# Passing a matmul's columns in turns: eight orders of the moving columns in 40 tiles of a two-layer expert network

## The chip, the cores and the metric

The kernel runs on one core of one Trainium2 chip. The metric is the device time of one execution in microseconds. Three runs of the kernel before gave 2364.71, 2369.80 and 2374.26 us, with a median of 2369.8 us.

## The reference, cut to what matters

A network of three blocks works on 256 tokens of width 1024 in float32. The part that matters here is the expert layer (`peer_ffn`), which stands behind each of the first two mixers. Every token picks 16 of 16384 experts for each of 8 heads; each expert is one row of `u` and one row of `v`:

```
u = u_tab[expert]
act = jax.nn.gelu(jnp.einsum('thkd,td->thk', u, xc).astype(jnp.float32), approximate=False)
w = (g * act).astype(xc.dtype)
return jnp.einsum('thk,thkd->td', w, v_tab[expert])
```

The kernel doesn't gather the rows. It computes the activations of all 16384 experts, multiplies them by gates that are zero for the experts not picked, and multiplies the result with the whole of `v`: out (256 x 1024) = w (256 x 16384) times v (16384 x 1024). This last product is the v stage.

## The kernel before, in words

All weights stream through one object (`Stream`, `self.ws`). A DMA on SP's queue brings a tile of 128 x 1024 float32 into `raw`; ScalarE copies it, rounded, into the first half of a `parts` buffer (line 103), and VectorE subtracts that from `raw` to give the rest (line 105). There are three `raw` and three `parts` buffers, used in turn. The moving operand of a product is 512 columns of such a part.

Each product of the reference is three products on TensorE (`mm3`, lines 464 to 468): high by high (466), high by low (467), low by high (468), all added up in one PSUM bank. `fp32r` in the profile is the type of the rounded parts.

In the v stage 128 tiles of `v` are taken one after another by `acc_tile`. For each tile the stationary operand is a block of 128 experts by 128 tokens of w, for two halves of the tokens (`tt`); the moving operand is the tile of `v`, in two halves of 512 columns (`hf`). That makes 2 x 2 x 3 = 12 products of 128x512 for a tile, and the sums stay in four PSUM banks of 512 float32 columns each until all 128 tiles are through. The stationary operands come from the array A by ScalarE (line 1124) and VectorE (line 1125), two tiles at a time. In the second half of the stage, which is the one changed, they lie in three pairs of tiles named w; in the first half four of five lie in hT. The second half runs through 60 tiles in the loop of lines 1104 to 1107 and through the last four in `close`.

Nothing here is scheduled by a planner: instructions stand on each engine in the order in which the Python code issues them. Ahead of each tile, `self.ws.get()` issues the splits and loads that are due.

## Time and profile before

| | |
|---|---|
| median of three runs | 2369.8 us (2364.71 to 2374.26) |
| the profiled execution | 2370.52 us |
| span of the profiled execution, first to last instruction | 2368.7 us |
| PE (TensorE matmul) busy | 2326.8 us, 98% of the span, 16813 products |
| DVE (VectorE) busy | 1767.5 us, 75% |
| ACT (ScalarE) busy | 1402.5 us, 59% |
| DMA | 406.90 MB, mean 172 GB/s |

A busy PE means that a product was under way: products are pipelined, so the time of one in the groups is its latency, and what a product costs is the distance from its start to the next one's start. PEld is the load of a stationary operand, which runs beside the products.

### The profile page before, as it was taken

The page shows a single profiled execution, that of the slowest core. Times are in us where ns is not written, and L with a number is a line of the kernel's source. Part 1 is how long each engine was busy: PE and PEld are TensorE (multiplying, and loading weights), DVE is VectorE, ACT ScalarE, POOL GpSimd, SP SyncE. Part 2 cuts the span into 40 slices and gives each one's busy share as a digit, 9 for nine tenths or more (in the row PEclk, how much of TensorE's full clock was granted, in tenths as well). Part 3 has the DMA queues.
Part 4 walks back from the last instruction along what each step waited for, and adds up shares of the span by engine and source line. Part 5 has one row for each costly group of instructions (what it writes and reads, how often), then busy time and mean ns, then how long its engine had stood idle before and what let it go on. Part 6 is the DMA issues. An engine that isn't in the chain of part 4 may idle for free.

```text
span 2368.7 us, 42927 instructions
## 1 busy us (share of the span) xinstructions
PE 2326.8 (98%) x16813; PEld 2082.1 (88%) x16814; DVE 1767.5 (75%) x3378; ACT 1402.5 (59%) x2109; POOL 144.3 (6%) x184
## 2 busy tenths in 40 slices
PE   9999999999999999999999999999999999999998
PEld 6679999999888888878999999888888899997987
DVE  6759997888999555557999788999755645548654
ACT  4554446777877445674445777877644555544543
POOL 1220000000000001121000000000000101215000
PEclk9899999999999999999999999999999999999999
DMA  5345555555555655434555555555556553435554
GB/s 179 107 134 162 191 186 178 177 177 175 183 177 178 197 194 194 157 106 161 169 195 190 183 175 178 181 177 177 197 194 195 177 168 114 158 119 177 187 193 153
DMA packets 113242, 406.90 MB, mean 172 GB/s; under 512 B 13200, under 2 KB 13584, under 8 KB 112784
## 3 DMA queue, kind: packets, MB, share of 16 engines
q1 hardware_dynamic: 112896, 403.91, 52.0%
q8 instruction: 131, 2.15, 0.4%
q14 instruction: 71, 0.58, 0.1%
q10 hardware_dynamic: 144, 0.26, 0.0%
HBM read 403.08 MB, written 1.05 MB: 171 GB/s over the span
## 4 chain that ended last, share of the span: by engine, by line
PE 84%; DVE 11%; issue 2%; ACT 2%; DMA 1%; POOL 1%; POOLq 0%; DVEq 0%; ACTq 0%
PE bank L466 25%; PE bank L468 25%; PE bank L467 25%; DVE parts L105 4%; PE bank L1174 3%; PE bank L740 1%; DVE ri L1211 1%; DVE ri L1214 1%; DVE rw L1212 1%; DVE rv L1213 1%; PE bank L783 1%; PE bank L810 1%; PE bank L739 1%; PE bank L526 1%; DVE rv L1210 1%
## 5 line engine op out<-in xcount | busy, mean ns | idle before, releaser
L105 DVE TENSOR_TENSOR parts<-raw,parts 128x1024 fp32r<-128x1024 f32 (+1 forms) x714 | 871.0, 1224 | 387.9 <-ACT parts L103 386.7
L103 ACT ACTIVATE parts<-raw 128x1024 fp32r<-128x1024 f32 (+2 forms) x726 | 759.3, 1050 | 474.0 <-PE bank L468 317.9
L468 PE MATMUL bank<-hT,parts 128*128 128x256 f32 x2816 | 783.4, 278 | 9.0 <-DVE parts L105 8.7
L466 PE MATMUL bank<-hT,parts 128*128 128x256 f32 x2816 | 789.6, 280 | 0.0
L467 PE MATMUL bank<-hT,parts 128*128 128x256 f32 x2816 | 781.4, 277 | 0.0
L468 PEld LDWEIGHTS bank<-hT,parts 128*128 128x128 f32 x2816 | 528.7, 188 | 12.6 <-DVE parts L105 12.5
L466 PEld LDWEIGHTS bank<-hT,parts 128*128 128x128 f32 x2816 | 529.0, 188 | 5.6 <-issue 3.5
L467 PEld LDWEIGHTS bank<-hT,parts 128*128 128x128 f32 x2816 | 531.8, 189 | 0.1
L466 PE MATMUL bank<-parts,hT 128*128 128x512 f32 (+4 forms) x624 | 240.6, 386 | 0.2 <-ACT parts L103 0.2
L467 PE MATMUL bank<-parts,hT 128*128 128x512 f32 (+4 forms) x624 | 235.9, 378 | 0.8 <-DVE parts L105 0.8
L468 PE MATMUL bank<-parts,hT 128*128 128x512 f32 (+4 forms) x624 | 236.1, 378 | 0.0
L466 PE MATMUL bank<-parts,w 128*128 128x512 f32 x592 | 230.9, 390 | 0.0
L468 PE MATMUL bank<-parts,w 128*128 128x512 f32 x592 | 230.4, 389 | 0.0
L467 PE MATMUL bank<-parts,w 128*128 128x512 f32 x592 | 230.3, 389 | 0.0
L1116 ACT ACTIVATE A<-bank 128x512 f32<-128x512 f32 x128 | 76.6, 598 | 180.4 <-PE bank L468 180.4
L1146 ACT ACTIVATE e<-i2T 128x512 f16<-128x512 f16 x256 | 157.5, 615 | 3.7 <-DVE o L1152 3.1
L1147 ACT ACTIVATE eg<-gT 128x512 f16<-128x512 f16 x256 | 157.4, 615 | 0.0
L466 PEld LDWEIGHTS bank<-parts,hT 128*128 128x128 f32 x624 | 117.3, 188 | 21.3 <-issue 1.7
L468 PEld LDWEIGHTS bank<-parts,hT 128*128 128x128 f32 x624 | 117.2, 188 | 20.8
L467 PEld LDWEIGHTS bank<-parts,hT 128*128 128x128 f32 x624 | 117.4, 188 | 19.9 <-DVE parts L105 1.1
L467 PEld LDWEIGHTS bank<-parts,w 128*128 128x128 f32 x592 | 111.1, 188 | 23.0
L468 PEld LDWEIGHTS bank<-parts,w 128*128 128x128 f32 x592 | 111.1, 188 | 23.0
(380 smaller groups left out, 2993.4 us busy)
## 6 DMA issues: line engine op xcount, KB each, us to landing
raw<-in_u_dram SPq DMA_DIRECT2D x256, 512.0 KB, 3.7
raw<-in_v_dram SPq DMA_DIRECT2D x256, 512.0 KB, 3.6
raw<-in_pq_dram SPq DMA_DIRECT2D x32, 512.0 KB, 3.6
raw<-in_w2g_dram SPq DMA_DIRECT2D x32, 512.0 KB, 3.6
raw<-in_w2u_dram SPq DMA_DIRECT2D x32, 512.0 KB, 3.7
raw<-in_w2d_dram SPq DMA_DIRECT2D x32, 512.0 KB, 4.3
raw<-in_w2t_dram SPq DMA_DIRECT2D x24, 512.0 KB, 3.5
raw<-in_w_dram SPq DMA_DIRECT2D x20, 512.0 KB, 4.0
```

The source lines that it names most:

```text
L103: self.nc.scalar.activation(hi[:, :n], r[:, :n], AF.Copy)
L105: engine.tensor_tensor(lo[:, :n], r[:, :n], hi[:, :n].bitcast(F32), op=OP.subtract)
L466: mm(out, sh, mh, start=start, stop=False)
L467: mm(out, sh, ml, start=False, stop=False)
L468: mm(out, sl, mh, start=False, stop=stop)
L526: self.nc.tensor.matmul(acc[:, :n], a, w[:, c], start=k + p == 0, stop=k == K - 1 and p == 2)
L739: nc.tensor.matmul(p[:, 0:128], qT[:, 0:128], kT[:, 0:128], start=True, stop=True)
L740: nc.tensor.matmul(p[:, 128:384], qT[:, 128:256], kT, start=True, stop=True)
L1116: self.nc.scalar.activation(A[:, i:i + 2, :], p.rearrange("p (c t) -> p c t", c=2), AF.Gelu)
L1146: nc.scalar.activation(e2, i2T[:, t, None].to_broadcast([128, B, 128]), AF.Copy)
L1147: nc.scalar.activation(eg.rearrange("p b (k i) -> p b k i", k=2), gT[:, t, :, None].to_broadcast([128, B, 2, HALF]), AF.Copy)
L1174: nc.tensor.matmul(p[:, j * HALF:(j + 1) * HALF], o2[:, j % B, :], og[:, j % B, k * HALF:(k + 1) * HALF], start=(k == 0), stop=(k == 1))
```

## The change: the order in which the columns pass

In 40 of the first 50 tiles of the v stage's second half, in layer 0 only, the moving operand and the PSUM output get a view that passes the same 512 columns in another order. An order (a, c) cuts the 512 columns into `a` streams of 512 / a columns that lie one behind the other; the streams take turns, `c` columns at a time. (2, 2) passes columns 0, 1, 256, 257, 2, 3, 258, 259 and so on; (16, 16) passes 0 to 15, 32 to 47, ..., 480 to 495, then 16 to 31, 48 to 63 and so on. Input and output are viewed alike, so each column's sum goes to the same place of the bank as before. Ten orders of five tiles each follow one another; `None` leaves the straight order.

```diff
+ORDERS = ((2, 2), None, (2, 8), (2, 16), (16, 2), None, (2, 32), (4, 16), (8, 32), (16, 16))
...
-    def acc_tile(self, acc, k, K, h, l):
+    def acc_tile(self, acc, k, K, h, l, order=None):
+
         wh, wl = self.ws.get()
+        turns = lambda t: t.rearrange("p (a b c) -> p b a c", a=order[0], c=order[1]) if order else t
...
-                self.mm3(acc[2 * tt + hf], h[:, t], l[:, t], wh[:, c], wl[:, c], k == 0, k == K - 1)
+                self.mm3(turns(acc[2 * tt + hf]), h[:, t], l[:, t], turns(wh[:, c]), turns(wl[:, c]), k == 0, k == K - 1)
...
-                self.acc_tile(acc, HALF + i, N_TILES, *act(i))
+                self.acc_tile(acc, HALF + i, N_TILES, *act(i), ORDERS[i // 5] if l == 0 and i < 50 else None)
```

TensorE's rows show it at two places; a row is line, operation, output bank and operands, and the shape of the moving operand, and the three lines of `mm3` repeat for each bank (`parts` holds the tile of `v`, w0 to w2 the stationary operands). At the end of the first order's five tiles, in the last tile's last two banks and the first product of the sixth tile, the kernel before has:

```order
L466 MATMUL bank7_82<-parts_71,w2_9273 128x512
L467 MATMUL bank7_82<-parts_71,w2_9273 128x512
L468 MATMUL bank7_82<-parts_71,w2_9273 128x512
L466 MATMUL bank4_79<-parts_71,w2_9273 128x512
L467 MATMUL bank4_79<-parts_71,w2_9273 128x512
L468 MATMUL bank4_79<-parts_71,w2_9273 128x512
L466 MATMUL bank5_80<-parts_71,w2_9273 128x512
```

The changed kernel has at the same place of TensorE's program (its lines are numbered three higher):

```order
L469 MATMUL bank7_82<-parts_71,w2_9273 128x128x2x2
L470 MATMUL bank7_82<-parts_71,w2_9273 128x128x2x2
L471 MATMUL bank7_82<-parts_71,w2_9273 128x128x2x2
L469 MATMUL bank4_79<-parts_71,w2_9273 128x128x2x2
L470 MATMUL bank4_79<-parts_71,w2_9273 128x128x2x2
L471 MATMUL bank4_79<-parts_71,w2_9273 128x128x2x2
L469 MATMUL bank5_80<-parts_71,w2_9273 128x512
```

No row moved: only the shape differs, 128 rounds of 2 streams with runs of 2 columns in place of one run of 512, and with the sixth tile the straight order is back. At the second place, where the fourth order hands over to the fifth, TensorE's rows of the changed kernel read:

```order
L469 MATMUL bank4_79<-parts_71,w0_9271 128x16x2x16
L470 MATMUL bank4_79<-parts_71,w0_9271 128x16x2x16
L471 MATMUL bank4_79<-parts_71,w0_9271 128x16x2x16
L469 MATMUL bank5_80<-parts_71,w1_9272 128x16x16x2
L470 MATMUL bank5_80<-parts_71,w1_9272 128x16x16x2
L471 MATMUL bank5_80<-parts_71,w1_9272 128x16x16x2
```

In the kernel before the same six rows are these:

```order
L466 MATMUL bank4_79<-parts_71,w0_9271 128x512
L467 MATMUL bank4_79<-parts_71,w0_9271 128x512
L468 MATMUL bank4_79<-parts_71,w0_9271 128x512
L466 MATMUL bank5_80<-parts_71,w1_9272 128x512
L467 MATMUL bank5_80<-parts_71,w1_9272 128x512
L468 MATMUL bank5_80<-parts_71,w1_9272 128x512
```

Here too nothing moved: 16 rounds of 2 streams with runs of 16 become, in the next tile, 16 rounds of 16 streams with runs of 2. The rows of the other engines are the same in both kernels.

## Rows read from the trace of the kernel before

**Rows 1.** The page: busy time, share of the span and instructions of each engine.

```profile
PE 2326.8 (98%) x16813; PEld 2082.1 (88%) x16814; DVE 1767.5 (75%) x3378; ACT 1402.5 (59%) x2109; POOL 144.3 (6%) x184
```

**Rows 2.** The page: the chain that ended last, by engine and by line.

```profile
PE 84%; DVE 11%; issue 2%; ACT 2%; DMA 1%; POOL 1%; POOLq 0%; DVEq 0%; ACTq 0%
PE bank L466 25%; PE bank L468 25%; PE bank L467 25%; DVE parts L105 4%; PE bank L1174 3%; PE bank L740 1%; DVE ri L1211 1%; DVE ri L1214 1%; DVE rw L1212 1%; DVE rv L1213 1%; PE bank L783 1%; PE bank L810 1%; PE bank L739 1%; PE bank L526 1%; DVE rv L1210 1%
```

**Rows 3.** Timeline, TensorE: start us, us, engine, line, operation, operands, count.

```profile
773.12 0.39 PE L468 MATMUL bank<-parts,hT 128*128 128x512 f32 x1
773.34 0.39 PE L466 MATMUL bank<-parts,w 128*128 128x512 f32 x1
773.57 0.39 PE L467 MATMUL bank<-parts,w 128*128 128x512 f32 x1
773.80 0.39 PE L468 MATMUL bank<-parts,w 128*128 128x512 f32 x1
774.02 0.39 PE L466 MATMUL bank<-parts,w 128*128 128x512 f32 x1
```

**Rows 4.** Windows: length, busy us (count) of each engine, clock, DMA.

```profile
core 0: us, PE busy (x) PEld busy (x) DVE busy (x) ACT busy (x) POOL busy (x), PEclk, DMA share, GB/s
773.30:786.90 13.60, 13.60 (x61) 11.26 (x61) 7.49 (x8) 6.86 (x8) 0.00 (x0) 1.00 0.70 231
786.90:800.50 13.60, 13.60 (x61) 11.26 (x61) 7.78 (x8) 6.34 (x7) 0.00 (x0) 1.00 0.59 193
...
895.70:909.30 13.60, 13.60 (x61) 11.26 (x61) 7.78 (x8) 6.34 (x7) 0.00 (x0) 1.00 0.58 193
773.30:909.30 136.00, 136.00 (x601) 112.61 (x601) 76.32 (x75) 65.99 (x75) 0.00 (x0) 1.00 0.60 197
```

**Rows 5.** Groups in 773.3 to 909.3 us: busy us, mean ns, idle before, releaser.

```profile
L466 PE MATMUL bank<-parts,w 128*128 128x512 f32 x200 | 77.8, 389 | 0.0
L467 PE MATMUL bank<-parts,w 128*128 128x512 f32 x200 | 77.8, 389 | 0.0
L468 PE MATMUL bank<-parts,w 128*128 128x512 f32 x200 | 77.8, 389 | 0.0
```

**Rows 6.** Waits in 773.3 to 909.3 us: who waited, total us, times, longest us.

```profile
ACT parts L103 <- PE bank L468: 68.6, 49, 1.7
DVE parts L105 <- ACT parts L103: 59.6, 50, 1.5
```

**Rows 7.** Timeline, TensorE's bf16 products at the program's start.

```profile
12.70 0.38 PE L443 MATMUL bank<-w 128*128 128x512 bf16 x1
15.77 1.46 PE L443 MATMUL bank<-w 128*128 128x512 bf16 x6
```

**Rows 8.** Lines L1159 and L1125 on VectorE: duration ns min/median/max.

```profile
L1159 DVE TENSOR_TENSOR A<-A,bank x128: 671/680/691, 402.9 to 1692.0; 128x512 f32<-128x512 f32 x128
L1125 DVE TENSOR_TENSOR w<-A,w x78: 681/684/691, 581.5 to 1858.1; 128x512 fp32r<-128x512 f32 x78
```

## The prediction

> **What bounds the kernel now.** I read the page's head first: the reader is to see that TensorE is busy for 2326.8 us of a span of 2368.7 us (98%), VectorE for 75% and ScalarE for 59% [rows 1]. The chain of work that ended last agrees: 84% of it is PE, and three quarters of the span lie on the three matmul lines of one helper, L466 to L468 [rows 2]. An average over stages could hide that the changed stage is bound otherwise, so I then cut out that stage. The v stage's second half works through tile after tile with stationary operands from the tiles named w; its first product starts at 773.34 us [rows 3]. The windows of 13.60 us from there on hold five tiles each, 60 products of 128x512 [rows 4]. [...] One product thus takes 136.00 us / 600 = 226.7 ns of the array, which the starts in the timeline show singly (773.34, 773.57, 773.80) [rows 3]. The 389 ns in the groups are the latency of one product, of which the next ones overlap a part [rows 5].

> Nobody keeps PE waiting there. The only waits in the stage are ScalarE's split waiting for PE to free a buffer of parts (68.6 us over 49 times) and VectorE's waiting for ScalarE [rows 6]. So every ns that a product gains or loses in this stage arrives whole at the end of the span; a slower PE only makes those two wait longer, and the DMA behind them with them. A faster PE could be followed: VectorE is idle for 59.7 of the 136.0 us, ScalarE for 70.0 [rows 4].

> **The change, part by part.** No instruction is added or removed and none changes its place, on any engine; the same 512 columns meet the same weights, and each result goes to the same place in the bank. What differs is the order of the columns within 480 products (8 orders x 5 tiles x 12). They fall into: 120 with runs of 2 columns, 60 with runs of 8, 180 with runs of 16, 120 with runs of 32. The ten tiles under None keep the straight order.

> The only cost there can be is the pace of these 480 products. At 226.7 ns they take 108.8 us now; to move the total by 0.5% (11.8 us, about what a measurement of this kernel can tell from no change), they must change by 24.7 ns each on the mean, 11%. No row of the trace shows a product whose columns are not one straight run, so I bound the price.

> [...]

> *From above:* the nearest row with a broken order is VectorE's product of A with the gates, L1159. It reads its bank with elements 64 apart and writes A in runs of 8, and takes 680 ns for 512 elements; the subtraction at L1125, which reads and writes straight runs, takes 684 [rows 8]. So on VectorE broken order costs nothing, but VectorE only has to handle 512 elements in 680 ns. If PE handled broken columns at no better than that pace, a product would lose 680 - 227 = 453 ns and the 480 would lose 218 us. That is the far end, without anything that speaks for it.

> [...]

> I take zero. [...]

> **The sum.** 2370.5 us of the profiled execution (span 2368.7 and 1.8 around it), plus 0 for instructions, plus 480 x 0. The profiled execution lies 0.7 us above the median of the three timed runs, 2369.8; I leave 0.5 us for small losses of the runs of two and forecast **2371 us**.

> **Rivals.**
> [...]
> 2. *Runs of two run at half pace* (slower). If what PE reads or writes at once is four columns wide, a run of two uses half of each piece: 512 columns take the time of 1024, 213 ns more for 120 products, 25.6 us: 2396 us. All longer runs are free. Nothing in the trace speaks for it except that PE's pace is three times VectorE's; against it, again, VectorE's strided rows.
> [...]
> [...]

> **How the numbers follow.** No price: 0.57. Rival 1: 0.17, rival 2: 0.12, rival 3: 0.10, rival 4: 0.04. The likeliest gives 2371. No price, rival 4 and rival 1 hold 0.78 together, so the range has to reach to rival 2: from 2362 (rival 4 less the scatter of the runs, which lie from 2364.7 to 2374.3) to 2397; about 0.12 stays outside. The likeliest one's own range is 2365 to 2376. Rival 1 lies at the edge of 0.5%, so somewhat over half of it counts as slower: slower 0.10 + 0.12 + 0.10 = 0.32, same 0.57 + 0.04 + 0.07 less 0.02 for a lucky set of runs = 0.66, faster 0.02.

> **What would show it.** In the windows of five tiles, if I am right, all ten still take 13.60 us and the stage ends where it did; the start-to-start time of products stays at 227 ns. [...] The prediction is wrong if any group of orders leaves 227 ns by more than some 25 ns on the mean of all, or if something outside the stage changes: a splitting engine or a DMA that reads the same memory and is slowed by the scattered reads.

## The result, and the profile after

The changed kernel takes 2390.72 us in the median of five runs (2387.21 to 2397.48), the kernel before 2369.8 us (2364.71 to 2374.26). The ratio is 1.0098, with an interval of 1.0079 to 1.0116: slower by 18.7 to 27.5 us. The page of the changed kernel has these lines for busy time and for the chain that ended last, which answer to [rows 1, 2]:

```profile
PE 2348.2 (98%) x16813; PEld 2084.5 (87%) x16814; DVE 1766.8 (74%) x3378; ACT 1402.1 (59%) x2109; POOL 144.7 (6%) x184
PE 84%; DVE 11%; ACT 2%; issue 2%; DMA 1%; POOL 1%; POOLq 0%; ACTq 0%; DVEq 0%
```

Only PE's busy time has moved, from 2326.8 to 2348.2 us; the shares of the chain are the same. The windows of the stage show where. Each is one order of the table, five tiles and 60 products, cut at the starts of the products, with the columns of [rows 4]; the sixth order, None, is left out, and the last row is all fifty tiles:

```profile
766.66:787.04 20.38, 20.38 (x61) 11.85 (x60) 7.93 (x8) 6.88 (x8) 0.00 (x0) 1.00 0.49 158
787.04:800.68 13.64, 13.64 (x61) 11.27 (x60) 7.33 (x7) 6.34 (x7) 0.00 (x0) 1.00 0.58 188
800.68:815.28 14.60, 14.60 (x62) 11.43 (x60) 7.73 (x8) 6.86 (x8) 0.00 (x0) 1.00 0.58 180
815.28:829.68 14.40, 14.40 (x61) 11.40 (x60) 7.53 (x8) 6.33 (x7) 0.00 (x0) 1.00 0.57 182
829.68:856.85 27.17, 27.17 (x61) 12.40 (x60) 7.93 (x8) 6.87 (x8) 0.00 (x0) 1.00 0.38 116
...
870.49:884.69 14.20, 14.20 (x62) 11.35 (x60) 7.66 (x8) 6.86 (x8) 0.00 (x0) 1.00 0.59 185
884.69:898.57 13.88, 13.88 (x61) 11.28 (x60) 7.60 (x8) 6.34 (x7) 0.00 (x0) 1.00 0.60 189
898.57:912.76 14.19, 14.19 (x61) 11.27 (x60) 7.65 (x8) 6.86 (x8) 0.00 (x0) 1.00 0.59 187
912.76:927.16 14.40, 14.40 (x62) 11.30 (x61) 7.61 (x8) 6.34 (x7) 0.00 (x0) 1.00 0.56 183
766.66:927.16 160.50, 160.50 (x602) 114.84 (x601) 76.30 (x75) 66.02 (x75) 0.00 (x0) 1.00 0.53 167
```

Before, each of these windows was 13.60 us long [rows 4]. Now the first, (2, 2), takes 20.38 us and the fifth, (16, 2), 27.17 us. The second and the sixth, where the order is None, are back at 13.64. The other six, with runs of 8 to 32 columns, take 13.88 to 14.60. The whole is 160.50 us in place of 136.00, 24.5 us more, of which the two orders with runs of 2 make 20.35 and the six longer ones 4.07. PE is busy without a gap in all of them, at a granted clock of 1.00. Only the pace of the products changed, as the timeline of PE shows in the first and the fifth order (start us, latency us):

```profile
767.32 0.51 PE L471 MATMUL bank<-parts,w 128*128 128x512 f32 x1
767.66 0.51 PE L469 MATMUL bank<-parts,w 128*128 128x512 f32 x1
...
840.08 0.63 PE L471 MATMUL bank<-parts,w 128*128 128x512 f32 x1
840.53 0.63 PE L469 MATMUL bank<-parts,w 128*128 128x512 f32 x1
```

One product starts 340 ns after the other in (2, 2) and 453 ns in (16, 2), where it was 227 [rows 3]. The waits of the stage, the answer to [rows 6], are those of a slower PE:

```profile
ACT parts L106 <- PE bank L471: 91.5, 49, 4.4
DVE parts L108 <- ACT parts L106: 83.9, 50, 4.2
```

ScalarE and VectorE wait longer for the same releases. The same stage of layer 1, which keeps the straight order, still takes 13.60 us for five tiles.

The span grew by 20.2 us, less than the 24.5 of the stage, because the stage began at 766.66 us instead of 773.34. The program ahead of it is the same in both kernels; in the runs below, this start lies between 762.7 and 774.1 us. It is scatter of that earlier part, not the change. The part behind the stage took 2.4 us more.

### The profile page after: what moved, and what is told of

It is laid out like the page before. It is cut to its first block, busy times and chain, and to the rows that moved or that the text cites. A ratio compares the mean times of both kernels' runs of the same rounds, so it can differ in the third digit from the quotient of the medians.

```text
span 2388.9 us, 42927 instructions
## 1 busy us (share of the span) xinstructions
PE 2348.2 (98%) x16813; PEld 2084.5 (87%) x16814; DVE 1766.8 (74%) x3378; ACT 1402.1 (59%) x2109; POOL 144.7 (6%) x184
## 4 chain that ended last, share of the span: by engine, by line
PE 84%; DVE 11%; ACT 2%; issue 2%; DMA 1%; POOL 1%; POOLq 0%; ACTq 0%; DVEq 0%
PE bank L469 26%; PE bank L471 25%; PE bank L470 25%; DVE parts L108 4%; PE bank L1179 3%; DVE ri L1216 1%; DVE ri L1219 1%; DVE rw L1217 1%; PE bank L745 1%; DVE rv L1218 1%; PE bank L788 1%; PE bank L529 1%; PE bank L815 1%; PE bank L744 1%; DVE rv L1215 1%
## 5 line engine op out<-in xcount | busy, mean ns | idle before, releaser
L471 PEld LDWEIGHTS bank<-hT,parts 128*128 128x128 f32 x2816 | 531.6, 189 | 11.8 <-DVE parts L108 11.6
L469 PE MATMUL bank<-parts,w 128*128 128x512 f32 x592 | 239.8, 405 | 0.0
L470 PE MATMUL bank<-parts,w 128*128 128x512 f32 x592 | 239.1, 404 | 0.0
L471 PE MATMUL bank<-parts,w 128*128 128x512 f32 x592 | 239.0, 404 | 0.0
L471 PEld LDWEIGHTS bank<-parts,w 128*128 128x128 f32 x592 | 111.9, 189 | 30.7 <-issue 4.9
L469 PEld LDWEIGHTS bank<-parts,w 128*128 128x128 f32 x592 | 111.9, 189 | 30.4 <-issue 4.9
L470 PEld LDWEIGHTS bank<-parts,w 128*128 128x128 f32 x592 | 111.9, 189 | 30.1 <-issue 4.9
L469 PEld LDWEIGHTS bank<-parts,hT 128*128 128x128 f32 x624 | 117.3, 188 | 21.3 <-issue 1.7
L471 PEld LDWEIGHTS bank<-parts,hT 128*128 128x128 f32 x624 | 117.2, 188 | 20.8
```

Of the source, the lines that this page charges most:

```text
L469: mm(out, sh, mh, start=start, stop=False)
L470: mm(out, sh, ml, start=False, stop=False)
L471: mm(out, sl, mh, start=False, stop=stop)
```

## The experiments

### Theories

The read: the moving operand would be fetched from SBUF in pieces, and short runs would waste part of a piece. The write: the bank would take columns in pieces. The generator: each jump from stream to stream would have its price, wherever it goes. All kernels below change only the tiles of the v stage's second half; a window is five tiles unless said otherwise, and a time per product is its length divided by 60. But for the two kernels whose time is given, each was run once, and what is read from it are the windows of that one trace, at a granted clock of 1.00.

### One side at a time

```diff
-    self.mm3(turns(acc[2 * tt + hf]), h[:, t], l[:, t], turns(wh[:, c]), turns(wl[:, c]), ...)
+    self.mm3(turns(acc[2 * tt + hf], out), h[:, t], l[:, t], turns(wh[:, c], read), turns(wl[:, c], read), ...)
```

An entry of the table is now a pair, the order of the write (`out`) and that of the read (`read`).

> The new order is put on one side of the product at a time, so the sums land in other columns than the reference's: in layer 0 the ten groups of five tiles take turns with the read of the moving operand alone and the write to PSUM alone, for (2, 2), (16, 2), (2, 8), (2, 16) and (16, 16); layer 1 does the same for (2, 32), (4, 16) and (8, 32), then (2, 2) and (16, 2) on both sides again. Theory R, the read: SBUF is read in pieces of four columns, and a run of two wastes half of each; then (16, 2) takes 453 ns a product with the read alone and 227 with the write alone, (2, 2) 340 and 227. Theory W, the write: the bank takes its columns in pieces wider than two; then it is the other way round. Theory G, the address generator: a jump costs time on either side; then both sides alone show part of it or each shows all of it. Layer 1 on both sides: 340 and 453 again if the price belongs to the order and not to the place in the program.

The windows of layer 0 (length, PE's busy time and count, clock, DMA), in pairs of read alone and write alone, for (2, 2), (16, 2) and, after the left-out (2, 8), (2, 16):

```profile
767.43:787.81 20.38, 20.38 (x61) 1.00 0.49 159
787.81:801.45 13.64, 13.64 (x62) 1.00 0.54 186
801.45:828.60 27.15, 27.15 (x61) 1.00 0.34 116
828.60:842.24 13.64, 13.64 (x61) 1.00 0.46 155
...
870.45:884.85 14.40, 14.40 (x62) 1.00 0.54 183
884.85:898.49 13.64, 13.64 (x61) 1.00 0.58 191
```

The read alone shows the whole price of each order: 20.38, 27.15, 14.60, 14.40 and 14.40 us, as in the change. The write alone shows none: 13.60 to 13.64. Layer 1 gives the same for the three remaining orders (read 14.20, 13.88 and 14.19 us, write 13.60, 13.63 and 13.64) and 20.39 us for (2, 2) on both sides again, but 28.17 for (16, 2) in place of 27.17. The theory of the write has fallen, and so has that of the generator in its form for either side. The eight orders of the write took no more than 13.64 us against the 13.60 of the straight order, pairs from 16 streams among them. Single columns were not tried.

### Other numbers of streams and other runs

```diff
+ORDERS = (((4, 2), (8, 2), (32, 2), (64, 2), (128, 2), (256, 2), (2, 4), (16, 4), (64, 4), (128, 4)),
+          ((16, 8), (64, 8), (4, 4), (4, 2)))
```

The table is written short: each order stands for the write and the read, the first line for layer 0, the second for layer 1.

> Both sides in turns as in the change, with other numbers of streams and other runs: runs of 2 with 4, 8, 32, 64, 128 and 256 streams, runs of 4 with 2, 16, 64 and 128; in layer 1 runs of 8 with 16 and 64 streams, then (4, 4) and (4, 2). With 256 streams of two columns, or 128 of four, there is one round only and the order is straight again: 227 ns under each theory, unless a pattern written with more dimensions costs by itself. Pieces of four columns without memory of the last ones: 453 ns for each number of streams with runs of 2, and 227 to 245 for runs of 4. Pieces that stay at hand for some streams: 340 for few streams and 453 for many, with a step between 2 and 16. A price for each jump whatever its length: runs of 4 take half the surplus of runs of 2, that is 283 ns with 2 streams and 340 with 16, and runs of 8 with 16 streams some 283.

The windows of (4, 2) and (8, 2), then of (128, 2), (256, 2), (2, 4) and (16, 4), in layer 0, and last that of (4, 4) in layer 1:

```profile
762.72:789.34 26.62, 26.62 (x61) 1.00 0.41 137
789.34:818.55 29.21, 29.21 (x61) 1.00 0.28 91
...
872.11:899.18 27.07, 27.07 (x61) 1.00 0.30 97
899.18:912.84 13.66, 13.66 (x61) 1.00 0.46 155
912.84:927.85 15.01, 15.01 (x61) 1.00 0.53 175
927.85:942.64 14.79, 14.79 (x61) 1.00 0.53 177
...
1785.29:1801.36 16.07, 16.07 (x61) 1.00 0.49 164
```

From four streams on, the length of the run decides: 26.62, 29.21, 25.88, 27.68 and 27.07 us for runs of 2 with 4, 8, 32, 64 and 128 streams, near twice the 13.60 of the straight order. (256, 2) is the straight order again and takes 13.66; the trace records its operand as one run of 512 columns, so it says nothing of what a pattern with more dimensions costs by itself. With runs of 4, which have half as many jumps, most is gone: 15.01 us with 2 streams, 14.79 with 16, 14.00 with 64. The exception is 4 streams, which keep 16.07 us, 268 ns, more than the 227 to 245 that were expected of pieces. A price for each jump can't be it all the same: it asked for 283 and 340 ns with 2 and 16 streams where 250 and 247 were measured, and these four orders have the same number of jumps at 233 to 268 ns. Between runs of 2 (8 bytes) and runs of 4 (16 bytes) lies a step: 340 to 487 ns on the one side, 233 to 268 on the other. The step from 340 to 443 ns lies between 2 and 4 streams. The forecast of one time for all numbers of streams, 453, missed the spread of 431 to 487 ns.

### The runs of 2 alone, and the others alone

```diff
-ORDERS = ((2, 2), None, (2, 8), (2, 16), (16, 2), None, (2, 32), (4, 16), (8, 32), (16, 16))
+ORDERS = ((2, 2), None, None, None, (16, 2), None, None, None, None, None)                      # one kernel
+ORDERS = (None, None, (2, 8), (2, 16), None, None, (2, 32), (4, 16), (8, 32), (16, 16))         # the other
```

The tables are again written short, each order for both sides.

> The change with the two orders of runs of 2 alone; the other six groups are straight. From the trace of the change: (20.20 - 13.60) + (26.76 - 13.60) = 19.8 us of the stage's 24.2 us, so a time some 19.8 us above the kernel before, ratio 1.008. If instead the many kinds of orders disturb each other, or the loss lies outside the stage, well under half of the change's loss.

> The change without the two orders of runs of 2: the six orders with runs of 8 to 32 remain. From the trace of the change: 14.60 + 14.82 + 14.19 + 13.89 + 14.19 + 14.37 less 6 x 13.60 = 4.5 us, ratio 1.002, which lies within 0.5%. If the loss of the runs of 2 came from what stands around them, 10 us or more would stay here.

The kernel before has a median of 2366.7 us here. The runs of 2 alone give 2387.43 us, ratio 1.0083 (1.0064 to 1.0103); the longer runs alone 2369.86 us, ratio 1.0013 (1.0001 to 1.0025). That is 19.6 and 3.1 us by the ratios; together 22.7, where the whole change has 23.2 by its own. The parts add up, and five sixths of the loss are ten tiles. The first expectation counted 20.20 and 26.76 us for the two orders of runs of 2 and the second 14.82 for (2, 16); cut at the starts of the products, these windows of the change are 20.38, 27.17 and 14.40 us, so 20.35 and 4.07 us were due in place of 19.8 and 4.5.

### Pieces of 16 bytes

If the fetch goes by aligned pieces of 16 bytes, a run of 4 must cost double when it is moved by two columns, and columns that are read again must cost nothing. The read takes one of these views; the shift goes two columns on in the first half of the tile and two columns back in the second, and both lie half a piece off:

```diff
+at = hf * 512 + (off - 4 * hf if off else 0)     # off: 0 or 2 columns
+w = w[:, at:at + 512]
+w.rearrange("p (a b c) -> p b a c", a=16, c=n)                           # turns
+w[:, 0:128].rearrange("p (a c) -> p a c", c=n)[:, :, None, :].to_broadcast([128, 128 // n, 4, n])   # again
```

> Only the read of the moving operand is changed, so the sums are others than the reference's. Theory P: the moving operand is fetched in aligned pieces of 16 bytes (4 columns of fp32), one in 226.7 / 128 = 1.77 ns, and the straight order is bound by these fetches, not by the array. Then a straight read two columns further on takes 227 ns (129 pieces), runs of 4 with 16 streams 247 where they lie on pieces and 453 two columns further on (256 pieces), runs of 8 some 245 and, two columns further on, 340 (192 pieces); 128 columns read four times in place of 512 stay at 227, and each group of 4 columns read four times in a row falls to 216 if a piece stays at hand and stays at 227 if not; pairs read four times in a row 216 or 453. Theory B, bursts of any four columns in a row: the shift by two columns changes nothing. Theory J, each jump has its price: a shift changes nothing either, and the repeated groups of 4 cost as many jumps as runs of 4, some 247.

The windows, in this order: straight two columns off; runs of 4 on the pieces, then two columns off; runs of 8 on the pieces, then two columns off; and, after the left-out runs of 2, each group of 4 columns four times in a row, the 128 columns four times over, each pair four times in a row and each group of 16 four times in a row:

```profile
763.78:777.79 14.01, 14.01 (x61) 1.00 0.67 221
777.79:792.58 14.79, 14.79 (x61) 1.00 0.56 182
792.58:818.98 26.40, 26.40 (x62) 1.00 0.35 118
818.98:832.81 13.83, 13.83 (x61) 1.00 0.46 154
832.81:854.19 21.38, 21.38 (x61) 1.00 0.40 130
...
881.37:894.34 12.97, 12.97 (x61) 1.00 0.49 160
894.34:907.96 13.62, 13.62 (x62) 1.00 0.58 195
907.96:920.90 12.94, 12.94 (x61) 1.00 0.61 203
920.90:934.79 13.89, 13.89 (x61) 1.00 0.58 191
```

Two columns off, the runs of 4 go from 14.79 to 26.40 us, 440 ns a product, and the runs of 8 from 13.83 to 21.38, 356 ns: close to what was expected of the 256 and 192 pieces that they touch, 453 and 340 ns, and far from bursts or jumps, which a shift can't change. The trace shows the times and no fetch: the pieces are the reading of them that fits best. Where each piece serves at least four times in a row, products run at 216 ns (12.97 and 12.94 us), the pace of six bf16 products, (1.46 - 0.38) us / 5 [rows 7], although the repeated pairs jump after every two columns. So I put the 11 ns that the straight fp32 order takes beyond that down to its fetches. The 128 columns four times over stay at 227 ns (13.62 us), and groups of 16, which are four pieces, take 231 (13.89 us): read so, a piece is not kept while three others are read. The miss is the straight read two columns off, 233.5 ns where 227 was expected.

That a fetch always takes 1.77 ns is not shown. (32, 2) would make 256 fetches in 431 ns, which is 1.68 ns each; at that pace 128 would take 216 ns, so the straight order's last 11 ns may have a second cause beside the number of its fetches.

### The same orders on bf16

```diff
+w = self.half_moved[:, c].rearrange("p (a b c) -> p b a c", a=order[0], c=order[1])
+s = self.ident_b
+self.mm3(acc[2 * tt + hf], s, s, w, w, k == 0, k == K - 1)
```

> In layer 0's first 50 tiles the products read a bf16 tile as moving operand and a bf16 identity as weights, in place of the tile of v and w, so the sums are others than the reference's; the write is straight. Theory P, pieces of 16 bytes at 1.77 ns each: 8 columns of bf16 fill a piece, so the straight order needs 64 pieces (113 ns) and the array sets its 216 ns; runs of 8 and more stay at 216, with 16 streams as with 2, since the fetch has room; runs of 4 need 128 pieces, 227; runs of 2 need 256, 453 with 16 streams and by the pattern of fp32 some 340 with 2. Theory C, four columns whatever their bytes: the straight order would be bound by 128 fetches, 227 ns, and runs of 8 would stay above. Theory J, each jump has its price: runs of 8 to 32 keep the surplus of 6 to 18 ns that they have in fp32.

PE's timeline in (16, 4) and in (16, 2):

```profile
828.25 0.38 PE L482 MATMUL bank<-half_moved,ident_b 128*128 128x512 bf16 x1
828.47 0.38 PE L480 MATMUL bank<-half_moved,ident_b 128*128 128x512 bf16 x1
...
849.59 0.61 PE L481 MATMUL bank<-half_moved,ident_b 128*128 128x512 bf16 x1
850.02 0.61 PE L482 MATMUL bank<-half_moved,ident_b 128*128 128x512 bf16 x1
```

Starts are 216 ns apart in (16, 4), 431 in (16, 2) and, by the same view, 271 in (2, 2). The straight order and all runs of 8 to 32 run at 216 as well, with 2 streams as with 16, and (2, 4) at 227. Where fp32 lost 4 to 17 ns with runs of 8 to 32, bf16 loses nothing. That fits a fetch with room, since eight columns of bf16 fill a piece; but the weights are bf16 here too, and in the kernel before the load of a bf16 tile of 128x128 takes PEld 98 ns (line 443, median of 42) where one of fp32 takes 188 (lines 466 to 468), so which of the two frees the longer runs isn't separated. Three numbers came out lower than 1.77 ns a piece (226.7 ns / 128) allows: 431 ns are 1.68 ns for each of 256 pieces, (16, 4) with its 128 pieces was expected at 227, and (2, 2) at some 340. And (2, 4) and (16, 4) touch equally many pieces at 227 and 216 ns, so the count alone doesn't set the time to within 11 ns.

### Two and four streams at other distances

```diff
+w = bass.AP(w.tensor, w.offset, [list(w.ap[0]), [n, 512 // (a * n)], [d, a], [1, n]])    # d columns from stream to stream
```

> Only the read is changed, so the sums are others than the reference's: two streams with runs of 2 columns, the second 4, 8, 16, 32, 64, 128 and 256 columns behind the first (256 is the change's (2, 2)), then four streams 4, 16 and 128 columns apart (128 is (4, 2)). Theory H: the last fetched piece or two are held, so that with two streams every other visit finds its piece; then all distances give 340 with two streams, and four streams 443 at any distance, except where neighbours share pieces (4 apart). Theory D: what counts is the distance, because places a certain step apart lie in one bank of SBUF; then two streams show other times than 340 at some of the distances, among 227 to 487.

The windows for two streams 4, 8 and 256 columns apart, and for four streams 4 and 128 apart:

```profile
770.40:783.50 13.10, 13.10 (x61) 1.00 0.72 239
783.50:803.10 19.60, 19.60 (x62) 1.00 0.44 140
...
881.80:901.50 19.70, 19.70 (x62) 1.00 0.40 133
901.50:925.12 23.62, 23.62 (x62) 1.00 0.36 122
...
951.52:978.12 26.60, 26.60 (x62) 1.00 0.31 99
```

From 8 to 256 columns, two streams take 19.60 to 19.70 us in all six cases, so the distance has no say. Only at 4 columns, where the two streams share their pieces, is the order free (13.10 us, 218 ns). Four streams cost more at each distance. That speaks for pieces that stay at hand for a moment, but the expectation's own sum doesn't follow from two held pieces: each of the 128 pieces is visited twice, so if every second visit found its piece, 128 fetches would remain, and 227 ns. The measured 327 to 340 are some 192 fetches of 1.70 to 1.77 ns, as if half of the second visits found theirs; which ones, and why, isn't shown. And the same read of (2, 2) that took 340 ns in three kernels takes 328 here, and 327 to 328 in the next kernel.

### Stationary tiles at other addresses

```diff
-act = self.v_act(A[1], [self.twins(tail, f"w{j}", 2) for j in range(3)])
+act = self.v_act(A[1], [self.twins(tail, f"w{j}", 2, 16 * j if l == 0 else 0) for j in range(3)])
```

> The stationary tiles of layer 0's second half lie 0, 64 and 128 bytes further on (first, second and third pair of w tiles, two tiles of v each in turn), and the orders stand in another sequence: straight, (2, 2), straight, (16, 2), (2, 16), (2, 8), (16, 16), (2, 2), (16, 2), straight. Theory P, the price is in the fetches of the moving operand alone: every order keeps its time in each tile, whichever w pair it reads and whatever stands before it: 227, 340, 227, 453, 240, 243.5, 240, 340, 453, 227 ns. Theory S, part of the price (the spread of 328 to 340 and of 453 to 473 seen for the same orders, the small surplus of the long runs, the 227 in place of 216) comes from weight loads that meet the fetches in the same place of SBUF: then tiles with the w pairs shifted show other times than those without, by 5 ns or more, in step with the pairs.

Windows of one tile (12 products): the straight order with w pairs 0, 64 and 128 bytes further on, then (16, 2) with 128, with 0 and with 64 bytes:

```profile
771.99:774.71 2.72, 2.72 (x13) 1.00 0.82 297
777.43:780.23 2.80, 2.80 (x13) 1.00 0.52 190
783.03:785.82 2.79, 2.79 (x13) 1.00 0.60 192
...
830.03:835.70 5.67, 5.67 (x13) 1.00 0.30 93
835.70:841.21 5.51, 5.51 (x13) 1.00 0.26 91
932.10:937.30 5.20, 5.20 (x13) 1.00 0.28 96
```

The straight order takes 2.72 us a tile on the pair that wasn't moved and 2.80 and 2.79 on the others, 226.7 against 233 ns. That holds in all three groups of straight tiles, so the place of the weights has a say there, as theory S asked. In (16, 2) it is only suggested: its ten tiles take 433 and 439 ns on the pair 64 bytes on, 457 to 465 on the pair that wasn't moved and 457 to 473 on the pair 128 bytes on. But the two fast tiles are the last of one group and the first of the other, and with no shift at all this order took 453 ns in the change and 470 in layer 1 of the first experiment. (2, 2) takes 328 ns on the unmoved pair too, so the pair's place doesn't explain its 340 elsewhere. Theory S does not hold for (2, 8), 243 ns on every pair, nor for (2, 16), 240 on every pair: the small price of the longer runs changes with neither shift that was tried.

## Why the prediction came out as it did

The range, 2362 to 2397 us, held the result only because it was stretched to rival 2, which had a chance of 0.12; the likeliest case, no price at all and 2371 us, did not happen. By its own sign the prediction was wrong: it allowed some 25 ns on the mean, and the 480 products left 227 ns by 24.4 us / 480 = 51 ns. What came, slower by more than 0.5%, had been given 0.32.

*What bounds the kernel* held. The stage is PE's from end to end, nothing else is late, and 24.5 us of slower products came out as 23.2 us by the timed ratio. No time was won either: no order that reads all 512 columns of fp32 was below 227 ns.

*Rival 2, half pace for runs of two*, was the mechanism for the larger part: 440 ns by its sum, 453 measured in (16, 2). In (2, 2) it was half the surplus, 340. Its 25.6 us became 20.35; the rest, 4.07 us, are the longer runs, which it held to be free. No run shows the 213 ns a product in its sum, from which the range has its upper end of 2397 us; in their place the runs showed 226 ns in (16, 2) and 113 in (2, 2). *Rival 1*, which had 0.17, asked the same price for each jump, so the same time in both orders of runs of 2, which have equally many jumps; measured were 340 and 453 ns. It is out, although it had the sign. That it lay at the edge of 0.5% came from a price of one clock cycle for a jump, and no run shows how long a cycle is; in its place the two orders of runs of 2 cost 20.35 us. *Rival 3*, which had 0.10, made anything but one straight run slow; it is excluded for the read by the six orders at 231 to 243 ns, and for the write by the experiment on the two sides. *Rival 4*, which had 0.04, was a gain from other meetings with the weight load, at best from 227 ns to the 216 of bf16 [rows 3, 7], 5.1 us for 480 products, from which the range has its lower end. It didn't come; the place of the weights does change times (227 to 233 ns in the straight order), but neither of the two shifts tried brought the straight order below 227.

The pieces of 16 bytes rest on the step between runs of 2 and runs of 4, 340 to 487 ns against 233 to 268, and on its move when the runs lie two columns off, where runs of 4 take 440 ns. Two columns from a piece at a time were not enough for the straight order's pace: pairs of fp32, read once, took 327 to 487 ns wherever the streams did not share their pieces.

What stays open: why 8 streams cost 487 ns and 32 streams 431, that is, why a piece, if pieces they are, takes 1.68 to 1.90 ns (431 and 487 ns / 256) in runs of 2 and 1.77 in the straight order; why 2 streams pay half of it; why (2, 2) takes 340 ns in some kernels and 328 in others; why runs of 4 cost most with 4 streams, 268 ns; and what exactly the longer runs lose in fp32, 4 to 17 ns, which isn't proportional to their number.

## What to carry to other kernels

Ask of the moving operand of a product how many 16-byte pieces of SBUF it touches, and whether broken orders cost it time: 128x512 in fp32 took 227 ns in the straight order and 231 to 243 in the change's runs of 8 to 32 columns, the same in bf16, with bf16 weights, 216 in both. The output in PSUM was written in pairs of fp32 from 16 streams at no cost (13.64 us for five tiles, straight 13.60), so where an order must change, try it on the write first and keep the read in straight runs that begin on a 16-byte boundary (226.7 ns, and 233.5 half a piece off). And a row is evidence for the memory and the run length that it has, not for the next shorter one.

## What the runs showed of the hardware that wasn't expected

A straight fp32 read that starts half a piece off takes 233.5 ns in place of 226.7. Stationary tiles 64 or 128 bytes further on cost a straight product 6 to 7 ns (2.80 and 2.79 us for 12 in place of 2.72). Re-reading saves time only at once: each group of 4 columns four times in a row runs at 216 ns, the same columns in four rounds at 227. Jumps that stay within a pair of columns cost nothing: pairs read four times in a row, a jump back after each, run at 216 ns.
